# Down projections set between the seven-product pairs, five of eight pairs in seven products, and x kept in DRAM

## The chip, the cores and the metric

The kernel runs on one core of a Trainium2 chip. The core has a matrix engine (TensorE, "PE" in the profile), a vector engine (VectorE, "DVE"), a scalar engine (ScalarE, "ACT"), a general engine (GpSimd, "POOL") and an engine that here only issues transfers (SyncE, "SP"). SP, ACT and POOL can each issue transfers between DRAM and the on-chip memory (SBUF). Matrix products land in eight accumulator banks (PSUM), each of 128 partitions by 512 f32 numbers. The metric is the device time of one execution in microseconds, as the median of several; lower is better.

## The reference

One encoder layer on 256 tokens of width 2048, all in f32. What matters here are its two feed-forward half-steps, which hold more than half of the time. Between them lies a mixing stage (pooling, dilated attention and cross-attention, gated and merged, then `W_out`).

```
x = x + 0.5 * (silu(h @ w_gate) * (h @ w_up)) @ w_down     # h = rmsnorm(x) * gain, d_ff = 5632
h = rmsnorm(x);  x = x + merged(h) @ w_out                  # three gated branches
x = x + 0.5 * (silu(h @ w_gate) * (h @ w_up)) @ w_down     # second half-step, own weights
out = rmsnorm(x) * final_norm
```

## The kernel before

**Products in three parts.** Every f32 operand is split into a high part (`wh`, rounded by an ACT copy to the matrix engine's f32r type) and a low part (`wl`, source minus high part, one DVE subtraction). A product of two 128-row blocks is three matmuls of 128x128 by 128x512: low by high, high by high, high by low. So one weight element costs one ACT pass, one DVE pass and three matmul passes per use.

**Weights.** A weight tile `wf` of 1 MB (128 x 4 x 512) is loaded by SP (L131, L146) into one of 3 buffers, and split into two halves of `wh` and `wl`, which rotate through 4 buffers each (`operands`, L118). An instruction that fills a buffer waits until the matmuls that read the buffer's previous tile are done.

**Feed-forward.** The 5632 hidden columns go in 11 chunks of 512 (`up`, L514). One chunk computes gate and up together, for 8 pairs of 128-row blocks of the 2048 input rows (`pair_gemm`, L221). A pair is either eight block products (two token halves by gate and up by two row blocks) or seven, by a Strassen-type scheme (`SEVEN_PRODUCTS`): the left side holds eight prepared blocks (`seven`), the right side needs the four weight blocks' sums (`sums`, three DVE additions, L153 to L155), which are split as well (`sumsh` on ACT L158, `sumsl` on DVE L159). Only three quarters of the weight tile itself is then split. The products accumulate over the pairs in eight banks q1 to q8, one bank for each product of the scheme. `finish` (L284) combines the banks into gate and up: q1 is copied by ACT, the rest are DVE additions. `SEVEN` = (0, 2, 4, 6): four of eight pairs take seven products, in chunk 0 one pair and in chunk 1 one pair.

**Down.** After silu and product, the chunk's result `u` is turned by the matrix engine (L379, eight 128x128 transposes into two banks) and split into `hT`. `STEPS` puts down(c) after up(c+1): four groups of 512 output columns, each 24 matmuls (4 row blocks, 2 token halves, 3 parts; `gemm`, L182 with L205 to L207) into two banks out of 0 to 3, and then one DVE instruction per token half that scales by 0.5 and adds to `X` (L550). The last two chunks go together in one down step. `X` (128 x 2 x 2048 f32, 16 KB of each partition) stays in SBUF from the first load to the end.

**Order.** The code is traced in program order, with small work items put in a list (`queue`) and taken from it between products (`pop`), and a scheduler then fixes one order for each engine. Each engine runs its own list strictly in order. Tiles with one tag share its buffers: `slot` has 14 of 8 KB (left sides, sums, `hT`), `tmp` 4 of 4 KB, `half` 2 of 2 KB.

Of the kernel before, what the change touches and what calls it, by code (L numbers as in the profile page):

```python
# [17 lines left out]
P = 128  # L18
S = 256
T = S // P  # L20
# [22 lines left out]
SEVEN = (0, 2, 4, 6)  # L43
QUARTERS = {3: (0,), 4: (1,), 5: (2,), 6: (3,)}

STEPS = (0, 1, *sum((((c, c + 1), c + 2) for c in range(9)), ()), (9, 11))
# [20 lines left out]
def tile_encoder_layer(ctx: ExitStack, tc: tile.TileContext, a: dict, out: bass.AP):  # L67
    nc = tc.nc
    sb = ctx.enter_context(tc.tile_pool(name="sb", bufs=1))
    ps = ctx.enter_context(tc.tile_pool(name="ps", bufs=1, space=bass.MemoryType.PSUM))  # L70
    count = [0]
# [149 lines left out]
    def pair_gemm(lhs, w, cols, order, sevens, out, after_seven=(), before=None, pieces=None):  # L221
# [44 lines left out]
        left = sum(7 if j in sevens else 8 for j in order)  # L266
        for j in order:
# [12 lines left out]
            if j == sevens[-1]:  # L280
                queue(*after_seven, soon=True)

    def finish(q, Q, out):


        (c11, c21), (c12, c22) = [[out[n][:, t] for t in range(T)] for n in range(2)]
        if q == "q1":
            nc.scalar.activation(c11, Q["q1"], AF.Copy)
        elif q == "q6":
            Q["v"] = half_tmp([P, CW], F32, "v")  # L290
            nc.vector.tensor_sub(Q["v"], Q["q6"], c11)
            nc.vector.tensor_sub(c21, Q["q7"], Q["v"])
            nc.vector.tensor_add(c12, Q["q5"], Q["v"])
            nc.vector.tensor_sub(c22, Q["q5"], c21)
        elif q not in ("q7", "q5"):
            c = {"q2": c11, "q4": c21, "q3": c12, "q8": c22}[q]
            nc.vector.tensor_add(c, Q[q], c)
# [21 lines left out]
    X = sb.tile([P, T, D], F32, name="X")  # L319
# [15 lines left out]
    def fill_pair(place, src, gain, early=False):  # L335

        seven, L = place
        if not seven:
            tile, half = L

            def part(k):
                j = 2 * half + k
                split(tile[:, 0, j], tile[:, 1, j], src()[:, k], gain[:, k : k + 1])

            return [lambda k=k: part(k) for k in range(2)]
        F = tmp([P, 8, P], "blocks")
# [15 lines left out]
        if early:  # L362
            def one(k):
                own(k)
                parts(slice(2 * k, 2 * k + 2))

            return [lambda: one(0), lambda: one(1), sums, lambda: parts(slice(4, 8))]
# [109 lines left out]
    xts = []  # L477

    def load_x(j):
# [5 lines left out]
        fill = fill_pair(lhs1[j], lambda: xt, g_ffn1[:, 2 * j : 2 * j + 2], early=j == 0)  # L485

        def part(k):
            nc.sync.dma_start(out=xt[:, k : k + step], in_=a["xT"][:, 2 * j + k : 2 * j + k + step, :])
            for f in fill[:1] if step == 1 else fill:
                f()  # L490
            del fill[:1]
            if step == 1 and k == 1:
                queue(*fill)

        def rows(q):
            t, half = q // 2, slice((q % 2) * D // 2, (q % 2 + 1) * D // 2)
            nc.sync.dma_start(out=X[:, t, half], in_=a["x"][t * P : (t + 1) * P, half])

            def squares():
                for n in (2 * (q % 2), 2 * (q % 2) + 1):  # L500
                    sumsq(ssq1, t, n, X[:, t, n * CW : (n + 1) * CW])

            queue(squares)
# [3 lines left out]


    def ffn(lhs, rstd, w_gate, w_up, w_down, after_chunk, operand=None, first=None, side={}):
# [4 lines left out]
        def up(c, after_down, before_down):  # L514
# [3 lines left out]
            kw = dict(before=first, pieces=lambda j: 1 if j == 0 else 2) if opening else {}  # L518
            g, u = tmp([P, T, CW], "gate"), tmp([P, T, CW], "up")
            sevens = SEVEN[-1:] if c == 0 else SEVEN[2::2] if c == 1 else SEVEN  # L520
            order = (1, 0, 3, 2, 5, 4, 6, 7) if after_down else range(KB // 2)
            pair_gemm(lhs, (w_gate, w_up), (c * CW, c * CW), order, sevens, (g, u), turns, **kw)
# [12 lines left out]
            hT[c], turns = turned_lhs(u, (4, 5) if before_down else (0, 1))  # L535
            if before_down:
                queue(*turns)
                turns = []

        def down(chunks, pieces, final):  # L540

            operands = [hT.pop(c) for c in range(*chunks)]
            for n in range(NCH):
                if pieces:
                    queue(*pieces[n], soon=True)
                acc = gemm(operands, w_down, chunks[0] * CW, n * CW, last=final and n == NCH - 1 and first is None)

                def residual(t, n=n, acc=acc):
                    xs = X[:, t, n * CW : (n + 1) * CW]
                    nc.vector.scalar_tensor_tensor(xs, acc[t], 0.5, xs, op0=ALU.mult, op1=ALU.add)  # L550
                    if final:
                        after_chunk(n, t)

                queue(*(lambda t=t, f=residual: f(t) for t in range(T)), soon=True)
                if final and operand is not None:
                    operand(n)

        for i, step in enumerate(STEPS):
            if isinstance(step, int):
                up(step, i > 0 and not isinstance(STEPS[i - 1], int), not isinstance(STEPS[i + 1], int))  # L560
            else:
                down(step, side.get(i, ()), i == len(STEPS) - 1)
# [101 lines left out]
    def side_work():  # L664
        return {len(STEPS) - 1: mem_pieces()}

# [3 lines left out]
    def after1(n, t):  # L670
        src = X[:, :, n * CW : (n + 1) * CW]
        sumsq(ssq2, t, n, src[:, t])

    def operand1(n):
        src = X[:, :, n * CW : (n + 1) * CW]
# [6 lines left out]
        operand1, first=load_x, side=side_work(),  # L682
# [309 lines left out]
    for n in range(NCH):  # L992
        acc = gemm(merged_lhs, a["w_out"], 0, n * CW)
        xs = X[:, :, n * CW : (n + 1) * CW]

        def residual(t, n=n, acc=acc, xs=xs):
            nc.vector.tensor_add(xs[:, t], acc[t], xs[:, t])
            sumsq(ssq3, t, n, xs[:, t])
# [11 lines left out]
    def after2(n, t):  # L1010
# [6 lines left out]
        sumsq(ssq4, t, n, X[:, t, c])  # L1017
        nc.vector.tensor_mul(XG[t][:, c], X[:, t, c], gf[:, c])
# [104 lines left out]
```

## Time and profile before

| | |
|---|---|
| median of 3 runs | 2362.07 us (2361.9 to 2362.45) |
| profiled execution, its own time | 2362.68 us |
| its span, first to last instruction | 2360.9 us |
| PE busy | 2348.3 us, 99% of the span |
| DVE busy | 1854.4 us, 79% |
| ACT busy | 1208.4 us, 51% |
| POOL busy | 0.7 us, no transfers issued |
| granted TensorE clock | 0.999 |

The profile lists, for each engine, the time in which it was busy, the groups of like instructions with the mean duration of one, and what ended each idle stretch. PE's matmuls overlap each other, so the duration of one (some 0.39 us) is not what one costs; the distance between starts is. An engine that is idle costs nothing as long as PE is not kept waiting by it.

### The profile page before, as it was taken

To read this page: it belongs to the slowest core of one execution; us is meant where nothing else is said; L and a number is where in the kernel's file an instruction comes from. 1 tells how busy PE (TensorE), PEld (TensorE's weight loads), DVE (VectorE), ACT (ScalarE), POOL (GpSimd) and SP (SyncE) were. 2 spreads that over 40 slices of the span, in tenths; PEclk is the share of its full clock that TensorE was granted. 3 is DMA by queue.
4 is the path that set the end of the run, shared out by engine and by line. 5 is a ranking of instruction groups with operands and counts; after the bars stand their busy time and mean duration, and the time that the engine had idled before them with its cause. 6 is when DMAs were issued, how large, how long until landed. Compare 5 with 4: busy or idle time off the path is not lost.

```text
span 2360.9 us, 27305 instructions
## 1 busy us (share of the span) xinstructions
PE 2348.3 (99%) x10325; PEld 1890.7 (80%) x10325; DVE 1854.4 (79%) x2282; ACT 1208.4 (51%) x1421; POOL 0.7 (0%) x6
## 2 busy tenths in 40 slices
PE   9999999999999999999999999999999999999998
PEld 7888888888888888888878888787888888888886
DVE  7788888988877676757777656876788888888886
ACT  7555555555556445543344454455555555555554
POOL 0000000000000000000000000000000000000000
PEclk9999999999999999999999999999999999999999
DMA  7555555555574555555545555555555555555563
GB/s 282 200 196 196 196 196 191 187 193 196 195 261 168 194 181 197 183 201 186 189 177 196 169 178 189 186 184 184 187 192 191 192 191 196 196 196 195 194 196 146
DMA packets 92916, 455.89 MB, mean 193 GB/s; under 512 B 10608, under 2 KB 11888, under 8 KB 61552
## 3 DMA queue, kind: packets, MB, share of 16 engines
q1 hardware_dynamic: 92496, 453.10, 56.7%
q8 instruction: 81, 1.33, 0.2%
q10 hardware_dynamic: 288, 1.05, 0.1%
q14 instruction: 51, 0.42, 0.0%
HBM read 452.01 MB, written 2.10 MB: 192 GB/s over the span
## 4 chain that ended last, share of the span: by engine, by line
PE 99%; DVE 0%; DMA 0%; ACT 0%; issue 0%; SPq 0%
PE acc L206 19%; PE acc L207 19%; PE acc L205 19%; PE q L231 13%; PE q L230 13%; PE q L229 13%; PE bank L379 1%; PE bank L822 0%; PE bank L748 0%; PE bank L713 0%; DMA xt<-in_xT 0%; PE bank L806 0%; PE bank L972 0%; PE bank L929 0%; PE bank L952 0%; PE bank L926 0%
## 5 line engine op out<-in xcount | busy, mean ns | idle before, releaser
L110 ACT ACTIVATE wh<-wf 128x1024 fp32r<-128x1024 f32 (+1 forms) x834 | 846.4, 1018 | 978.0 <-PE acc L206 562.5
L111 DVE TENSOR_TENSOR wl<-wf,wh 128x1024 fp32r<-128x1024 f32 (+1 forms) x834 | 970.1, 1169 | 410.0 <-ACT wh L110 405.0
L205 PE MATMUL acc<-wh,lhs 128*128 128x512 f32 x1920 | 769.8, 401 | 0.0
L206 PE MATMUL acc<-wh,lhs 128*128 128x512 f32 x1920 | 759.8, 396 | 0.0
L207 PE MATMUL acc<-wl,lhs 128*128 128x512 f32 x1920 | 758.7, 395 | 0.8 <-DVE wl L111 0.8
L207 PEld LDWEIGHTS acc<-wl,lhs 128*128 128x128 f32 x1920 | 360.4, 188 | 88.8 <-DVE wl L111 2.2
L205 PEld LDWEIGHTS acc<-wh,lhs 128*128 128x128 f32 x1920 | 360.7, 188 | 88.0 <-DVE lhs L111 0.3
L206 PEld LDWEIGHTS acc<-wh,lhs 128*128 128x128 f32 x1920 | 361.0, 188 | 80.2
L231 PE MATMUL q<-wl,lhs 128*128 128x512 f32 x704 | 280.2, 398 | 0.0
L229 PE MATMUL q<-wh,lhs 128*128 128x512 f32 x704 | 278.1, 395 | 0.0
L230 PE MATMUL q<-wh,lhs 128*128 128x512 f32 x704 | 278.0, 395 | 0.0
L158 ACT ACTIVATE sumsh<-sums 128x1024 fp32r<-128x1024 f32 x152 | 160.2, 1054 | 55.0 <-DVE sums L155 51.1
L159 DVE TENSOR_TENSOR sumsl<-sums,sumsh 128x1024 fp32r<-128x1024 f32 x152 | 185.3, 1219 | 0.0
L229 PEld LDWEIGHTS q<-wh,lhs 128*128 128x128 f32 x704 | 132.4, 188 | 32.8
L230 PEld LDWEIGHTS q<-wh,lhs 128*128 128x128 f32 x704 | 132.2, 188 | 33.0
L231 PEld LDWEIGHTS q<-wl,lhs 128*128 128x128 f32 x704 | 132.2, 188 | 31.4 <-DVE wl L111 0.5
L229 PE MATMUL q<-wh,seven 128*128 128x512 f32 x324 | 129.0, 398 | 2.0 <-ACT wh L110 1.5
L231 PE MATMUL q<-wl,seven 128*128 128x512 f32 x324 | 128.3, 397 | 0.0
L230 PE MATMUL q<-wh,seven 128*128 128x512 f32 x324 | 128.1, 396 | 0.0
L230 PE MATMUL q<-sumsh,seven 128*128 128x512 f32 x304 | 120.2, 395 | 0.0
L229 PE MATMUL q<-sumsh,seven 128*128 128x512 f32 x304 | 119.2, 392 | 0.0
L231 PE MATMUL q<-sumsl,seven 128*128 128x512 f32 x304 | 118.6, 391 | 0.0
(157 smaller groups left out, 1562.8 us busy)
## 6 DMA issues: line engine op xcount, KB each, us to landing
wf<-in_w_in SPq DMA_DIRECT2D x100, 1024.0 KB, 4.9
wf<-in_ffn_w_down SPq DMA_DIRECT2D x88, 1024.0 KB, 4.8
wf<-in_ffn_w_gate SPq DMA_DIRECT2D x175, 512.0 KB, 4.2
wf<-in_ffn_w_up SPq DMA_DIRECT2D x175, 512.0 KB, 5.2
wf<-in_w_mem_kv SPq DMA_DIRECT2D x16, 1024.0 KB, 4.8
wf<-in_w_out SPq DMA_DIRECT2D x16, 1024.0 KB, 4.8
wf<-in_w_up_pool SPq DMA_DIRECT2D x8, 1024.0 KB, 4.8
wf<-in_w_up_mem SPq DMA_DIRECT2D x8, 1024.0 KB, 4.8
```

The costliest lines, as they stand in the source:

```text
L110: nc.scalar.activation(hi, src, AF.Copy)
L111: nc.vector.tensor_sub(lo, src, hi.bitcast(F32))
L158: nc.scalar.activation(th[:, r], sums[:, r], AF.Copy)
L159: nc.vector.tensor_sub(tl[:, r], sums[:, r], th[:, r].bitcast(F32))
L205: nc.tensor.matmul(parts[t], lo, wh[:, k % 2], start=kb == 0, stop=False)
L206: nc.tensor.matmul(parts[t], hi, wh[:, k % 2], start=False, stop=False)
L207: nc.tensor.matmul(parts[t], hi, wl[:, k % 2], start=False, stop=kb == n - 1)
L229: nc.tensor.matmul(Q[q], lhsl, wh, start=first, stop=False)
L230: nc.tensor.matmul(Q[q], lhsh, wh, start=False, stop=False)
L231: nc.tensor.matmul(Q[q], lhsh, wl, start=False, stop=final)
L379: nc.tensor.transpose(state["b"][:, k, t * P : (t + 1) * P], src[:, t, c : c + P], ident)
```

## The change

- Five of eight pairs take seven products (`SEVEN` = 1, 2, 3, 5, 6), and they come first in a chunk, the three pairs of eight products last. Chunk 0 takes eight products in all pairs, chunk 1 seven in two pairs. Pair 1's left-side sums are made in chunk 1 instead of chunk 0.
- The down projection of chunk c is cut into eight pieces (4 column groups by 2 token halves, 12 matmuls each), set between products of the seven-product pairs of up(c+2). Each piece accumulates in bank 7 (q8's bank, which the seven-product pairs do not use), is copied by ACT with the factor 0.5 into a 2 KB `half` tile `y`, and POOL issues a transfer of 256 KB that adds `y` to x in DRAM.
- `X` no longer stays in SBUF. x lives in eight DRAM tiles; the first rows are written there by POOL, and the last down step and the `W_out` step read 512 columns at a time into `tmp` tiles by SP (`x_chunk`), add, and write back by POOL (not after the last step).
- The freed space gives `wh` and `wl` 6 buffers each instead of 4.
- Where a bank's chunk had no seven-product pair, ACT copies the bank out instead of a DVE addition.

```diff
-SEVEN = (0, 2, 4, 6)
+SEVEN = (1, 2, 3, 5, 6)
+SUMS = {5: 1}
+HID = DFF // CW
+BETWEEN = 4
...
-        return [sb.tile([P, 2, CW], F32R, tag=tag, bufs=4, name=nm(tag)) for tag in ("wh", "wl")]
+        return [sb.tile([P, 2, CW], F32R, tag=tag, bufs=6, name=nm(tag)) for tag in ("wh", "wl")]
...
+        places = [BETWEEN + (7 * len(sevens) - 1 - BETWEEN) * i // max(1, len(between) - 1) for i in range(len(between))]
...
+                done += 1
+                while places and done >= places[0]:
+                    places.pop(0)
+                    between.pop(0)()
...
-            nc.vector.tensor_add(c, Q[q], c)
+            if "q1" in Q:
+                nc.vector.tensor_add(c, Q[q], c)
+            else:
+                nc.scalar.activation(c, Q[q], AF.Copy)
...
-    X = sb.tile([P, T, D], F32, name="X")
+    XD = [[dr.tile([P, CW], F32, name=f"x{n}{t}") for t in range(T)] for n in range(NCH)]
...
+    def x_chunk(n):
+        xs = tmp([P, T, CW], "xs")
+        for t in range(T):
+            nc.sync.dma_start(out=xs[:, t], in_=XD[n][t])
+        return xs
...
-            sevens = SEVEN[-1:] if c == 0 else SEVEN[2::2] if c == 1 else SEVEN
-            order = (1, 0, 3, 2, 5, 4, 6, 7) if after_down else range(KB // 2)
+            sevens = () if c == 0 else SEVEN[1::2] if c == 1 else SEVEN
+            order = [j for j in range(KB // 2) if j not in sevens]
+            order = range(KB // 2) if c < 2 else [*sevens, *order]
+            between = down_pieces(c - 2) if c > 1 else ()
...
+        def down_pieces(c):
+            L = hT.pop(c)
+            W = {}
+            def piece(n, t):
+                if t == 0:
+                    W[n] = weights(w_down, c * CW, n * CW)
+                b = psum(7, [P, CW], "down")
+                for k in range(4):
+                    wh, wl = W[n][k // 2]
+                    hi = L[:, 0, k, t * P : (t + 1) * P]
+                    lo = L[:, 1, k, t * P : (t + 1) * P]
+                    nc.tensor.matmul(b, lo, wh[:, k % 2], start=k == 0, stop=False)
+                    nc.tensor.matmul(b, hi, wh[:, k % 2], start=False, stop=False)
+                    nc.tensor.matmul(b, hi, wl[:, k % 2], start=False, stop=k == 3)
+                y = half_tmp([P, CW], F32, "y")
+                nc.scalar.activation(y, b, AF.Copy, scale=0.5)
+                nc.gpsimd.dma_start(out=XD[n][t], in_=y, accum_op=ALU.add)
+            return [lambda n=n, t=t: piece(n, t) for n in range(NCH) for t in range(T)]
...
-                    xs = X[:, t, n * CW : (n + 1) * CW]
-                    nc.vector.scalar_tensor_tensor(xs, acc[t], 0.5, xs, op0=ALU.mult, op1=ALU.add)
+            xs = x_chunk(n)
+                nc.vector.scalar_tensor_tensor(xs[:, t], acc[t], 0.5, xs[:, t], op0=ALU.mult, op1=ALU.add)
...
+        nc.gpsimd.dma_start(out=XD[n][t], in_=xs[:, t])
```

**Where it moves instructions.** PE, in the middle of a chunk of the first half-step. Before, the down step stood between two chunks, two banks in turn (`acc`); its first rows, behind the last rows of the chunk's pair of eight products:

```order
L230 MATMUL q_5026<-wh_5286,lhs_86 128x512
L231 MATMUL q_5026<-wl_5287,lhs_86 128x512
L205 MATMUL acc_5321<-wh_5325,lhs_4821 128x512
L206 MATMUL acc_5321<-wh_5325,lhs_4821 128x512
L207 MATMUL acc_5321<-wl_5326,lhs_4821 128x512
```

Now a piece (`down`, 12 matmuls, its first and last three here) stands between the last product of pair 3 and the first of pair 5:

```order
L233 MATMUL q_1442<-wh_1545,seven_94 128x512
L234 MATMUL q_1442<-wl_1546,seven_94 128x512
L597 MATMUL down_1598<-wh_1590,lhs_844 128x512
L598 MATMUL down_1598<-wh_1590,lhs_844 128x512
L599 MATMUL down_1598<-wl_1591,lhs_844 128x512
...
L597 MATMUL down_1598<-wh_1592,lhs_844 128x512
L598 MATMUL down_1598<-wh_1592,lhs_844 128x512
L599 MATMUL down_1598<-wl_1593,lhs_844 128x512
L232 MATMUL q_1392<-wh_1627,seven_95 128x512
```

The twelve matmuls of a piece moved from a stretch of 96 into eight places among the products, and all of them use one bank.

ACT, the second half of the same seven-product pairs. Before, ACT's list there held only splits of weights and sums and, at the end, q1's copy:

```order
L158 ACTIVATE sumsh_5198<-sums_5194 128x1024
L110 ACTIVATE wh_5204<-wf_5191 128x1024
L110 ACTIVATE wh_5206<-wf_5191 128x512
L158 ACTIVATE sumsh_5240<-sums_5236 128x1024
L110 ACTIVATE wh_5246<-wf_5233 128x1024
```

Now the copies out of bank 7 (`y<-down`) stand between the splits:

```order
L601 ACTIVATE y_1611<-down_1598 128x512
L160 ACTIVATE sumsh_1679<-sums_1675 128x1024
L112 ACTIVATE wh_1701<-wf_1699 128x1024
L112 ACTIVATE wh_1703<-wf_1699 128x1024
L601 ACTIVATE y_1660<-down_1647 128x512
L112 ACTIVATE wh_1767<-wf_1764 128x1024
L112 ACTIVATE wh_1769<-wf_1764 128x1024
L300 ACTIVATE gate_1696<-q_1392 128x512
L601 ACTIVATE y_1722<-down_1709 128x512
```

`wf_1699` is the weight tile of the fourth column group of down, `wf_1764` that of pair 0. Each `y` waits for the end of a piece on PE, and what stands below it waits behind it.

SP, the last down step of the first half-step. Before:

```order
L131 DMA wf_5659<-in_ffn_w_down 128x2048
L635 DMA mem_5492<-in_mem 128x2048
L131 DMA wf_5711<-in_ffn_w_down 128x2048
L131 DMA wf_5775<-in_w_mem_kv 128x2048
L131 DMA wf_5815<-in_w_mem_kv 128x2048
```

Now, with the third and fourth group's x (`xs<-x`) and the last two of four column loads of the memory tokens (`xt<-in_memT`) among the first weights of the mixing stage:

```order
L133 DMA wf_5951<-in_ffn_w_down 128x2048
L694 DMA mem_5722<-in_mem 128x2048
L546 DMA xs_5760<-x_87 128x512
L546 DMA xs_5760<-x_88 128x512
L697 DMA xt_5841<-in_memT 128x1024
L133 DMA wf_6015<-in_w_mem_kv 128x2048
L133 DMA wf_6057<-in_w_mem_kv 128x2048
L697 DMA xt_5843<-in_memT 128x1024
L546 DMA xs_5892<-x_89 128x512
```

`xs` and `xt` share the four `tmp` buffers, so these loads wait for a buffer, and the weight loads below them wait on SP behind them.

More of the change, by code (lines that the diff above doesn't have):

```diff
@@ L219, in tile_encoder_layer, with pair_gemm @@
     BANK = {"q1": 0, "q6": 1, "q7": 2, "q5": 3, "q2": 4, "q4": 5, "q3": 6, "q8": 7}
-    def pair_gemm(lhs, w, cols, order, sevens, out, after_seven=(), before=None, pieces=None):
+    def pair_gemm(lhs, w, cols, order, sevens, out, after_seven=(), before=None, pieces=None, between=()):
         pop(1)
@@ L266, in pair_gemm @@
         left = sum(7 if j in sevens else 8 for j in order)
+        done = 0
+        between = list(between)
+        places = [BETWEEN + (7 * len(sevens) - 1 - BETWEEN) * i // max(1, len(between) - 1) for i in range(len(between))]
         for j in order:
@@ L277, in pair_gemm @@
                     finish(q, Q, out)
+                done += 1
+                while places and done >= places[0]:
+                    places.pop(0)
+                    between.pop(0)()
                 if left:
                     pop(left)
-            if j == sevens[-1]:
+            if sevens and j == sevens[-1]:
                 queue(*after_seven, soon=True)
     def finish(q, Q, out):
+        if not out:
+            out.extend(tmp([P, T, CW], name) for name in ("gate", "up"))
         (c11, c21), (c12, c22) = [[out[n][:, t] for t in range(T)] for n in range(2)]
@@ L333, in pair_tiles, with fill_pair @@
         return tiles
[L335 removed]
+    def fill_pair(place, src, gain, own_only=False, own_there=False):
         seven, L = place
@@ L345, in fill_pair, with straight @@
             return [lambda k=k: part(k) for k in range(2)]
+        if own_only:
+            def straight(k):
+                view = src()[:, k].rearrange("p (t c) -> p t c", t=T)
+                split(L[:, 0, 2 * k : 2 * k + 2], L[:, 1, 2 * k : 2 * k + 2], view, gain[:, k : k + 1])
+            return [lambda k=k: straight(k) for k in range(2)]
         F = tmp([P, 8, P], "blocks")
@@ L360, in parts @@
             split(L[:, 0, r], L[:, 1, r], F[:, r])
[L362 to L367, printed above, removed]
+        if own_there:
+            return [lambda: own(0), lambda: own(1), sums, lambda: parts(slice(4, 8))]
         return [lambda: own(0), lambda: own(1), sums, lambda: parts(slice(0, 8))]
@@ L534, in up @@
             queue(*(lambda t=t, f=f: f(t) for t in range(T) for f in (silu, product)), soon=True)
-            hT[c], turns = turned_lhs(u, (4, 5) if before_down else (0, 1))
-            if before_down:
+            hT[c], turns = turned_lhs(u, (0, 1) if c < HID - 1 else (4, 5))
+            if c == HID - 1:
                 queue(*turns)
[L538 to L548, printed above, removed]
-                    xs = X[:, t, n * CW : (n + 1) * CW]
[L550 to L556, printed above, removed]
@@ new lines, in ffn, with residual @@
+        for c in range(HID):
+            up(c)
+        operands = [hT.pop(c) for c in (HID - 2, HID - 1)]
+        for n in range(NCH):
+            if side:
+                queue(*side[n], soon=True)
+            xs = x_chunk(n)
+            acc = gemm(operands, w_down, (HID - 2) * CW, n * CW, last=n == NCH - 1 and first is None)
+            def residual(t, n=n, acc=acc, xs=xs):
+                nc.vector.scalar_tensor_tensor(xs[:, t], acc[t], 0.5, xs[:, t], op0=ALU.mult, op1=ALU.add)
+                after_chunk(n, t, xs)
+            queue(*(lambda t=t, f=residual: f(t) for t in range(T)), soon=True)
+            if operand is not None:
+                operand(n, xs)
```

63 lines of the change are left out of this document (35 added, 28 removed).

## The prediction

> **What bounds the kernel now.** I read the engines' shares first, then the chain of waits, then who keeps PE waiting.
>
> ```profile
> span 2360.9 us, 27305 instructions
> PE 2348.3 (99%) x10325; PEld 1890.7 (80%) x10325; DVE 1854.4 (79%) x2282; ACT 1208.4 (51%) x1421; POOL 0.7 (0%) x6
> PE 99%; DVE 0%; DMA 0%; ACT 0%; issue 0%; SPq 0%
> PE q L229 <- ACT wh L110: 1.5, 2, 1.2
> PE idle L308 <- DVE idle L305: 1.3, 1, 1.3
> PE acc L207 <- DVE wl L111: 0.8, 1, 0.8
> PE q L229 <- DVE gate L297: 0.5, 1, 0.5
> ```
>
> The page gives PE 99% of the span, and the chain that ends last is PE throughout. The last four rows are all of PE's waits (total, times, longest): 4.1 us in the whole kernel. A change therefore gains only what it takes from PE's list, and loses whatever it makes PE wait. What PE's list costs per matmul shows in the timeline and in the table by stretches (length, then busy time and count of PE, PEld, DVE, ACT, POOL):
>
> ```profile
> 394.73 0.39 PE L229 MATMUL q<-wh,lhs 128*128 128x512 f32 x1
> 423.39 0.39 PE L205 MATMUL acc<-wh,lhs 128*128 128x512 f32 x1
> 394.73:423.39 28.66, 28.66 (x124) 23.10 (x123) 24.78 (x28) 16.37 (x18) 0.00 (x0) 1.00 0.58 189
> 423.39:488.62 65.23, 65.23 (x285) 52.57 (x284) 57.30 (x65) 34.37 (x37) 0.00 (x0) 1.00 0.59 194
> ```
>
> Between the first two rows lie 123 matmul starts: 28.66 / 123 = 0.233 us each, at full granted clock (1.00). One whole round (down of one chunk, up of another) is the last row: 65.23 us, PE never idle, 276 matmuls (60 products x 3, and 96) at 0.233 = 64.3, and 8 transposes for the rest. DVE is busy 57.3 of it: 88%, the next bound.
>
> **The change, part by part.**
>
> *Removed from PE.* Per half-step, before: chunks 0 and 1 with 63 products each, nine with 60: 666. Now 64, 62 and nine with 59: 657. Nine products less, three matmuls each, two half-steps: 54 x 0.233 = **12.6 us**. Down and the transposes keep their counts. The round becomes 65.23 - 0.70 = 64.5 us.
>
> *DVE and ACT in a round.* Durations:
>
> ```profile
> L111 DVE TENSOR_TENSOR wl<-wf,wh 128x512 fp32r<-128x512 f32 x4 | 2.7, 682 | 0.0
> L159 DVE TENSOR_TENSOR sumsl<-sums,sumsh 128x1024 fp32r<-128x1024 f32 x8 | 9.7, 1218 | 0.0
> L550 DVE SCALAR_TENSOR_TENSOR X<-acc,X 128x512 f32<-128x512 f32 x8 | 5.2, 682 | 0.0
> L153 DVE TENSOR_TENSOR sums<-wf 128x1024 f32<-128x1024 f32 x4 | 4.9, 1226 | 0.7 <-DMA wf<-in_ffn_w_up 0.6
> L154 DVE TENSOR_TENSOR sums<-sums,wf 128x512 f32<-128x512 f32 x4 | 2.7, 684 | 0.0
> L110 ACT ACTIVATE wh<-wf 128x1024 fp32r<-128x1024 f32 x20 | 21.2, 1060 | 24.8 <-PE q L230 10.7 <-PE acc L206 8.7 <-issue 5.4
> L110 ACT ACTIVATE wh<-wf 128x512 fp32r<-128x512 f32 x4 | 2.5, 620 | 0.8 <-ACT sumsh L158 0.8
> L288 ACT ACTIVATE gate<-q 128x512 f32<-128x512 f32 x1 | 0.6, 577 | 0.0
> ```
>
> One more pair in seven products costs DVE one L153, two L154-like and two L159, and spares half of a 1024-wide L111: 1.23 + 1.37 + 2.44 - 0.54 = +4.5 us. The eight L550 go: -5.2. DVE stays at 57.3 - 0.7 = 56.6 of 64.5, 88% again. ACT gets eight copies like L288 (4.6) and 2 x 1.06 - 0.44: 34.4 + 6.3 = 40.7 of 64.5. So neither is a bound over a round; both are hidden under PE, and the price is nothing as long as each item is in time. That I check along one round, with t = 0 at the first matmul of pair 1, a product 0.70, a piece 12 x 0.233 = 2.80. The pieces then start at 2.8, 8.4, 14.0, 19.6, 25.9, 31.5, 37.1 and 43.4; the pairs of seven end at 46.9.
>
> *The copies out of bank 7 (ACT).* Each must be over before the next piece starts. The hand-over:
>
> ```profile
> 415.45 0.39 PE L231 MATMUL q<-sumsl,seven 128*128 128x512 f32 x1
> 415.95 0.69 DVE L291 TENSOR_TENSOR v<-q,gate 128x512 f32<-128x512 f32 x1 [0.72 <-PE q L231]
> ```
>
> The reader starts 0.50 after the last matmul's start, 0.27 after PE's next slot. A copy is thus over 0.27 + 0.58 = 0.85 us after its piece, and the next piece is 2.8 or 3.5 us away (four or five products). What can stand before it on ACT is a split that waits for its own buffer: the sixth piece's copy stands behind both splits of the fourth column group, and the second of these takes a buffer that this same piece reads to its end at 34.3. So 34.3 + 0.27 + 1.06 + 0.58 = 36.2, against 37.1: **0.9 us to spare**, the narrowest place. Behind that split comes its DVE part (1.22, so 36.9) for a matmul at 39.0. The copy of the last piece stands behind pair 4's and the first of pair 7's splits: 46.9 + 0.27 + 2 x 1.06 + 0.58 = 49.9, against q8's first product at 51.1. Nothing is late by these rows: cost 0; bounds 0 and, if each of 18 rounds loses the 0.9 it has, 16 us.
>
> *Weights for the pieces.* Six `wh` buffers are three tiles ahead instead of two, but a round still has twelve tiles of 1 MB (8 + 4) in 3 `wf` buffers.
>
> ```profile
> wf<-in_ffn_w_down SPq DMA_DIRECT2D x88, 1024.0 KB, 4.8
> bg<-in_b_gate SPq DMA_DIRECT2D x12, 256.0 KB, 3.2
> X<-in_x SPq DMA_DIRECT2D x4, 512.0 KB, 8.3
> xt<-in_memT SPq DMA_DIRECT2D x4, 512.0 KB, 6.8
> ```
>
> A tile comes 4.8 us after its buffer is free; when I follow DVE's new list with the durations above, buffers are free at t = -1.9 (for pair 3, whose sums should start at 6.9) and 6.9 (for the third column group, wanted by ACT at 14.0) leave over 2 us. Cost 0.
>
> *The adding transfers.* No transfer is issued by POOL before, so their time is bounded: 3.2 (the 256 KB row) from below, 8.3 (512 KB, in the crowded opening) from above; bytes move three times, so I take 5. Two `half` buffers alternate, and the tightest reuse is the last piece's: y of the seventh is read at 40.8, its transfer must land, the copy takes 0.6, q8 wants bank 7 at 51.1. So it holds up to 51.1 - 0.7 - 40.8 = **9.6 us**. DVE's `v` waits for the sixth's transfer (36.2 + 5 = 41.2, against q6's end at 42.0) with pair 4's splits behind it, which are wanted from 53 on. Cost 0 at 5 us. They add 8 x 256 KB to 12 MB per round, on engines that are 59% busy.
>
> The Trainium skill, "SBUF — State Buffer", Who interferes with whom, speaks against POOL as issuer: its descriptors cannot be written while a DVE instruction runs in a mode with both ports. But it says that additions of two tensors have no such mode, and a DVE row of 1024 elements here takes 1.22 us and one of 512 0.68, as without one. By the rule the transfers would start without delay, by its opposite up to one DVE row (1.2 us) late; 5 or 6.2 us, either is under 9.6.
>
> *x in DRAM at the edges.* In the last down step `xs` and the memory's `xt` share four buffers, with weights behind them on SP:
>
> ```profile
> 684.32 0.39 PE L205 MATMUL acc<-wh,lhs 128*128 128x512 f32 x1
> 711.07 21.24 SPq L131 DMA_DIRECT2D wf<-in_w_mem_kv x4
> 707.10 0.48 DVE L114 SCALAR_TENSOR_TENSOR lhs<-bank,gains,lhs 128x256 fp32r<-128x256 f32 x1
> 718.37 0.48 DVE L114 SCALAR_TENSOR_TENSOR lhs<-bank,gains,lhs 128x256 fp32r<-128x256 f32 x1
> 726.42 1.66 DVE L114 SCALAR_TENSOR_TENSOR lhs<-xt,gains,lhs 128x256 fp32r<-128x256 f32 x4
> ```
>
> The step starts at 684.3; the first x columns are done with at about 707 (last split of their transposed blocks), the second at about 718. The third `xs` can be issued at 707, before the mixing stage's first weights are due (711.1). The fourth `xt` waits until 718 and lands at 718 + 6.8 = 725; DVE's last use of such columns began at 726. Cost 0, upper bound one landing, 6.8. In the `W_out` step every load has 96 matmuls (22 us) of cover.
>
> *Opening.* Chunk 0 makes no weight sums and one ACT instruction less per first half tile (0.5 us), but PE then stands before the up weights, which land at 9.6 as before:
>
> ```profile
> 9.61 0.63 ACT L110 ACTIVATE wh<-wf 128x512 fp32r<-128x512 f32 x1 [0.72 <-DMA wf<-in_ffn_w_up]
> 11.09 0.44 PE L231 MATMUL q<-wl,seven 128*128 128x512 f32 x1
> ```
>
> Cost 0, between -0.4 and +1. The end keeps its chain.
>
> *Sum.* Against the profiled execution's own 2362.68: -12.6, all else 0, so 2350.1. It ran 0.6 above the median of 2362.07; so **2349.5** for the median.
>
> **The rivals.** *Copies late.* If ACT's list runs later than I reckon, each round loses at the pieces. For: ACT now waits for PE eight times per round, and had no such place. Against: the spare times above. At 0.7 us per round, 18 x 0.7 = 12.6 eats the gain (2362); at the full 0.9 it is 2349.5 + 16 = 2366, at the same place twice 2382.
>
> *Transfers too slow (other side).* One mechanism: y's buffer is not free, ACT stands at the next copy, bank 7 stays full, PE stands at q8. It decides from 9.6 us per adding transfer; each us above costs one per round: at 12 us 18 x 2.4 = 43, so 2393. For: three moves of the bytes, and the 8.3 us row. Against: the 3.2 row.
>
> *Edges.* If the fourth `xt` is late by its landing, 6.8 once: 2356.
>
> *No gain on PE.* If matmuls into one bank were spaced wider than 0.233, the pieces' 96 x 18 would lose. The rows of `acc` take two banks, but a product of `q` accumulates three in a row in one bank at that spacing; so I give it no chance of its own.
>
> **How the numbers follow.** Forecast (2348.5 to 2353) 0.60; edges and small stalls (2353 to 2357) 0.10; copies late 0.18, of which 0.11 ends within 0.2% and 0.07 slower; transfers too slow 0.12, slower. A measurement here can tell about 0.2%, 4.7 us, from no change. So faster 0.70, same 0.11, slower 0.19. The range reaches from 2348 to the 2366 of the copies and leaves out the transfers' case.
>
> **What would show it.** Right: PE 99%, 9711 matmuls of 128x512, a round of 64.5 us with PE not idle, PE's waits below 6 us in all, `y` copies within 0.9 us of their piece, adding transfers landing in 3 to 8 us. Wrong: PE waiting in `down` rows for `y` (copies), in q8's first product for `y` and ACT for transfers (second rival), SP's weight loads waiting behind `xs` near 710 us (edges). A gain above 14 us would mean that PE's spacing changed.

## The result, and the profile after

The changed kernel takes 2348.8 us (median of 4, 2348.36 to 2349.38) against 2362.0 for the kernel before on the same chip (4 runs, 2361.9 to 2362.45): a ratio of 0.9944, with a 95% interval of 0.9932 to 0.9957. It is faster by 13.2 us (0.6%); the forecast was 2349.5.

The page of the changed kernel (engines, and the shares of the chain that ended last):

```profile
span 2347.0 us, 27962 instructions
PE 2334.9 (99%) x10271; PEld 1877.0 (80%) x10271; DVE 1827.2 (78%) x2218; ACT 1311.8 (56%) x1609; POOL 138.5 (6%) x174
PE 99%; DMA 0%; DVE 0%; SPq 0%; ACT 0%; issue 0%; DVEq 0%; ACTq 0%
```

PE still has 99% of the span and 99% of the chain. It runs 54 matmuls fewer than before (10325 then), and the span is 13.9 us shorter. All that PE waits for in this kernel:

```profile
PE q L232 <- ACT wh L112: 2.1, 2, 1.5
PE idle L323 <- DVE idle L320: 1.3, 1, 1.3
```

3.4 us, where it was 4.1. Neither of the two rows has to do with a piece, a copy or a transfer. One round, from the first transpose of a chunk to that of the next, in the table by stretches (columns as in the prediction):

```profile
337.84:402.41 64.57, 64.57 (x282) 51.80 (x281) 56.25 (x62) 39.92 (x47) 6.92 (x8) 1.00 0.77 228
```

PE fills it without a gap; DVE has 56.25 us of it (it had 57.30 of 65.23), ACT 39.92 (34.37), and POOL, which had nothing, 6.92 for eight transfers. The DMA engines are 77% busy where they were 59%. The sixth piece of a round, its copy, the transfer that adds it, and what follows, in rows chosen from the timeline (start, duration, engine; in brackets the idle time before and what ended it):

```profile
259.76 0.40 PE L599 MATMUL down<-wl,lhs 128*128 128x512 f32 x1
260.93 0.58 ACT L601 ACTIVATE y<-down 128x512 f32<-128x512 f32 x1
261.81 0.86 POOL L602 DMA_DIRECT2D x<-y  x1 [5.44 <-ACT y L601]
262.81 0.39 PE L597 MATMUL down<-wh,lhs 128*128 128x512 f32 x1
...
265.85 0.60 ACT L601 ACTIVATE y<-down 128x512 f32<-128x512 f32 x1 [1.96 <-PE down L599]
266.75 0.86 POOL L602 DMA_DIRECT2D x<-y  x1 [4.08 <-ACT y L601]
267.45 0.39 PE L234 MATMUL q<-sumsl,seven 128*128 128x512 f32 x1
268.28 0.69 DVE L303 TENSOR_TENSOR v<-q,gate 128x512 f32<-128x512 f32 x1 [3.43 <-DMA x<-y]
```

The copy is over at 261.51, and the bank is wanted again at 262.81: 1.30 us to spare. DVE stands 3.43 us before `v`, but most of that is the written order: `v` reads q6, whose last matmul starts at 267.45, so it could not start before 267.95 (0.50 us behind the matmul, as in the prediction's rows). Only the last 0.33 us are the transfer: `v` takes the `half` buffer of this sixth `y`, and the transfer lands at 267.97, 6.2 us after its issue. PE does not notice. Nor does it notice ACT's wait before the last `y` of each round, whose buffer the seventh transfer still reads:

```profile
ACT y L601 <- DMA x<-y: 22.6, 18, 3.2
```

That copy is over 0.5 to 3.3 us before bank 7 is wanted by q8. The transfers of this kernel, with the median time from issue to landing at the end:

```profile
wf<-in_ffn_w_down SPq DMA_DIRECT2D x88, 1024.0 KB, 5.3
x<-y POOLq DMA_DIRECT2D x144, 256.0 KB, 6.4
```

### The profile page after: what moved, and what is told of

It is laid out like the page before. It is cut to its first block, busy times and chain, and to the rows that moved or that the text cites. A ratio compares the mean times of both kernels' runs of the same rounds, so it can differ in the third digit from the quotient of the medians.

```text
span 2347.0 us, 27962 instructions
## 1 busy us (share of the span) xinstructions
PE 2334.9 (99%) x10271; PEld 1877.0 (80%) x10271; DVE 1827.2 (78%) x2218; ACT 1311.8 (56%) x1609; POOL 138.5 (6%) x174
## 4 chain that ended last, share of the span: by engine, by line
PE 99%; DMA 0%; DVE 0%; SPq 0%; ACT 0%; issue 0%; DVEq 0%; ACTq 0%
PE acc L208 13%; PE acc L207 13%; PE acc L209 13%; PE q L232 13%; PE q L233 13%; PE q L234 13%; PE down L598 6%; PE down L599 6%; PE down L597 6%; PE bank L396 1%; PE bank L877 0%; PE bank L803 0%; PE bank L768 0%; DMA wf<-in_ffn_w_gate 0%; PE bank L861 0%; PE bank L1027 0%
## 5 line engine op out<-in xcount | busy, mean ns | idle before, releaser
L113 DVE TENSOR_TENSOR wl<-wf,wh 128x1024 fp32r<-128x1024 f32 (+1 forms) x834 | 951.9, 1159 | 362.8 <-ACT wh L112 358.8
L207 PE MATMUL acc<-wh,lhs 128*128 128x512 f32 x1344 | 537.7, 400 | 0.0
L208 PE MATMUL acc<-wh,lhs 128*128 128x512 f32 x1344 | 534.3, 398 | 0.0
L209 PE MATMUL acc<-wl,lhs 128*128 128x512 f32 x1344 | 528.4, 393 | 0.0
L207 PEld LDWEIGHTS acc<-wh,lhs 128*128 128x128 f32 x1344 | 252.5, 188 | 64.7 <-DVE lhs L113 0.3
L209 PEld LDWEIGHTS acc<-wl,lhs 128*128 128x128 f32 x1344 | 252.3, 188 | 60.6
L208 PEld LDWEIGHTS acc<-wh,lhs 128*128 128x128 f32 x1344 | 252.7, 188 | 54.3
L161 DVE TENSOR_TENSOR sumsl<-sums,sumsh 128x1024 fp32r<-128x1024 f32 x188 | 228.1, 1220 | 11.2 <-ACT sumsh L160 10.3
L598 PE MATMUL down<-wh,lhs 128*128 128x512 f32 x576 | 228.5, 397 | 0.0
L599 PE MATMUL down<-wl,lhs 128*128 128x512 f32 x576 | 228.0, 396 | 0.0
L597 PE MATMUL down<-wh,lhs 128*128 128x512 f32 x576 | 227.5, 395 | 0.0
L232 PE MATMUL q<-wh,lhs 128*128 128x512 f32 x528 | 222.1, 421 | 2.1 <-ACT wh L112 2.1
L233 PE MATMUL q<-wh,lhs 128*128 128x512 f32 x528 | 208.3, 395 | 0.0
L602 POOL DMA_DIRECT2D x<-y x144 | 124.6, 865 | 1156.6 <-ACT y L601 1136.3
L601 ACT ACTIVATE y<-down 128x512 f32<-128x512 f32 x144 | 85.3, 592 | 138.1 <-PE down L599 79.7
L233 PE MATMUL q<-sumsh,seven 128*128 128x512 f32 x376 | 148.7, 395 | 0.0
```

The lines of the kernel that those rows point to most:

```text
L113: nc.vector.tensor_sub(lo, src, hi.bitcast(F32))
L161: nc.vector.tensor_sub(tl[:, r], sums[:, r], th[:, r].bitcast(F32))
L207: nc.tensor.matmul(parts[t], lo, wh[:, k % 2], start=kb == 0, stop=False)
L208: nc.tensor.matmul(parts[t], hi, wh[:, k % 2], start=False, stop=False)
L209: nc.tensor.matmul(parts[t], hi, wl[:, k % 2], start=False, stop=kb == n - 1)
L232: nc.tensor.matmul(Q[q], lhsl, wh, start=first, stop=False)
```

## The experiments

Each time stands beside that of the kernel before in the same session (2361.8 to 2362.1 there). "Theory" and "rival" are those of the expectations.

**The fifth pair undone** (four of eight pairs in seven products; the pieces, the transfers and x in DRAM stay).

```diff
-SEVEN = (1, 2, 3, 5, 6)
+SEVEN = (1, 2, 3, 5)
```

> The pieces and the adding transfers stay; the fifth pair in seven products is undone (four of eight), so the eight pieces stand within 27 products and mostly three products (2.1 us) apart instead of four or five. Theory (the gain is the products taken from PE, and moving down costs nothing): 18 products more, 18 x 0.70 = 12.6 us, so 2348.8 + 12.6 = 2361.4, PE's waits as few as with five pairs. Rival (pieces in bank 7, x in DRAM or the six buffers give a part of the gain themselves, or cost something that the fifth pair hides): clearly under 2359 or over 2364.

Measured: 2445.2 us (2443.4 to 2450.3), 84 us over the 2361.4 of the theory and slower than the kernel before by 3.55% (3.40 to 3.71). Eighteen products cannot cost that. Its longest wait of PE; then rows of its timeline around 202 us (POOL, DVE and q6's last matmul), and PE's in the next round:

```profile
PE down L597 <- DVE up L310: 49.4, 16, 4.0
```

```profile
201.58 0.86 POOL L602 DMA_DIRECT2D x<-y  x1 [4.70 <-ACT y L601]
...
202.26 1.23 DVE L113 TENSOR_TENSOR wl<-wf,wh 128x1024 fp32r<-128x1024 f32 x1 [0.21 <-ACT wh L112]
...
205.83 0.40 PE L234 MATMUL q<-sumsl,seven 128*128 128x512 f32 x1
...
210.08 0.69 DVE L303 TENSOR_TENSOR v<-q,gate 128x512 f32<-128x512 f32 x1 [6.59 <-ACT wh L112]
```

```profile
236.81 0.40 PE L234 MATMUL q<-sumsl,seven 128*128 128x512 f32 x1
240.31 0.77 PE L597 MATMUL down<-wh,lhs 128*128 128x512 f32 x1 [3.10 <-DVE up L310]
240.87 0.63 PE L598 MATMUL down<-wh,lhs 128*128 128x512 f32 x1
241.30 0.63 PE L599 MATMUL down<-wl,lhs 128*128 128x512 f32 x1
```

DVE stands for 6.59 us before `v`. Up to 206.33, 0.50 us behind q6's last matmul, it would stand there in any case; the other 3.75 us `v` lacks its buffer, which the transfer issued at 201.58 still reads: it landed 8.2 us after its issue, at 209.8. (The profile names an ACT split, but ACT's last one before was over at 202.2.) By the same working the transfer holds `v` up for 0.33 us in the changed kernel's round above, for 7.6 us in its 18 rounds together, and for 69 us here. Two things make the difference: q6 ends five products after the sixth piece instead of seven (1.4 us), and in this round the transfer takes 2 us longer. Behind `v` stand five splits, and in the next round PE finds bank 7 (q8) not yet added: 3.1 us, 16 times. That the late splits lead to the late addition is read from DVE's list, not shown by itself. The rows after it show a second loss: the next matmuls start 0.43 us apart instead of 0.233.

**The same, with a buffer of its own for `v`.**

```diff
-SEVEN = (1, 2, 3, 5, 6)
+SEVEN = (1, 2, 3, 5)
...
-            Q["v"] = half_tmp([P, CW], F32, "v")
+            Q["v"] = slot([P, CW], F32, "v")
```

> Four pairs in seven products as in the run with the fifth pair undone (2445.2), with one more edit: v no longer takes one of the two half buffers that the y tiles use, but a buffer of the large pool, where one is free with four such pairs. Theory (the 84 us lost there come from DVE's v, which stood 6.6 us a round behind a transfer that still read its buffer, so that the splits behind it came late): the loss goes, and what stays is the price of 18 products, 2348.8 + 12.6 = 2361.4. Rival (the four weight tiles of the pieces within 28 products instead of 35 come too fast for the wf buffers and the DMA): 2425 to 2445, DVE still waits for wf.

Measured: 2371.0 us (2367.3 to 2371.8). 74 of the 84 us come back with this one edit, so the shared buffers were the cause of most of it. `v` now waits for q6 alone:

```profile
DVE v L303 <- PE q L234: 52.5, 20, 2.9
```

The edit also takes ACT's waits for a transfer before the last `y` away (33.4 us in 18 rounds without it, 1.6 us with it), so it shows the sharing as the cause, not `v` by itself. A calm round of this kernel:

```profile
271.53:336.89 65.36, 65.36 (x285) 52.27 (x284) 52.67 (x57) 37.96 (x46) 6.90 (x8) 1.00 0.78 225
```

65.36 - 64.57 = 0.79 us over the changed kernel's round, PE full: the price of one product (0.70), nearly as forecast. 9.6 us are left over; some rounds take 66.5 us, with PE waiting 3.6 us in nine places for a copy `y` and 2.5 us in three for q8's addition. What makes those rounds late I didn't settle. The sign of the rival is there: DVE still stands 75.8 us, 49 times, for the weights `wf` (104.9 us in the run before, 5.8 in the changed kernel), so a part of the rest may be the rival's.

**The fifth pair alone** (the kernel before with one line changed; chunk 1 gets two such pairs by it).

```diff
-SEVEN = (0, 2, 4, 6)
+SEVEN = (1, 2, 3, 5, 6)
```

> The kernel before with five pairs in seven products and nothing else: down stays one stage, x stays in SBUF, four buffers for wh and wl. PE's list loses ten products per half-step (chunk 1 has 62): 60 x 0.233 = 14.0 us, so 2348.1 if nothing else bounds. Theory (the fifth pair needs the rest of the change, since the up stage alone would ask DVE for 37.3 + 4.5 = 41.8 us in 42.9 - 0.7 = 42.2): PE waits for DVE's sumsl and wl in every round; at one to three us each, 2348 + 18 to 54 = 2366 to 2402. Rival (the buffers smooth it over the stages, DVE has 61.8 of 64.5 us over a round): 2348 to 2352, and the moving of down was not needed for the gain.

Measured: 2349.6 us (2348.8 to 2350.7), a ratio of 0.9947 (0.9932 to 0.9962); no difference from the whole change can be told. The theory fell, the rival holds. The round and the waits of PE:

```profile
297.77:362.29 64.52, 64.52 (x283) 52.00 (x281) 61.14 (x70) 35.88 (x39) 0.00 (x0) 1.00 0.58 196
```

```profile
PE q L229 <- DVE seven L111: 2.1, 1, 2.1
PE idle L308 <- DVE idle L305: 1.3, 1, 1.3
PE q L229 <- DVE X L550: 0.9, 1, 0.9
PE q L229 <- ACT wh L110: 0.4, 1, 0.4
```

DVE is busy 61.14 of 64.52 us, 95%, and PE is still full in nearly every round (the third wait, 0.9 us, is the only one inside a round). A likely reason, read from the rows, is that the buffers carry DVE's surplus of the up stage over into the down stage. So the fifth pair by itself gives the gain. The rest without it is the first run above, and costs 83 us. Added to the fifth pair, it brings little or nothing: this kernel's list is 6 matmuls (1.4 us) shorter than the changed kernel's, and 1.5 us of its forecast of 2348.1 are missing, so the rest could be worth a us or two, which these runs can't tell from nothing. What it does bring is room, 56.25 us on DVE instead of 61.14.

**Four buffers instead of six.**

```diff
-        return [sb.tile([P, 2, CW], F32R, tag=tag, bufs=6, name=nm(tag)) for tag in ("wh", "wl")]
+        return [sb.tile([P, 2, CW], F32R, tag=tag, bufs=4, name=nm(tag)) for tag in ("wh", "wl")]
```

> wh and wl get four buffers each again instead of six. The span gained 13.9 us where the 54 matmuls explain 12.6; PE's three gaps of 0.67, 0.98 and 0.42 us (at 51, 1196 and 13 us of the span before) are gone. Theory A (the 0.98 us at 1196 us, in the mixing stage that the change doesn't touch, went because of the two more buffers): PE waits there again for DVE's wl, the time is 2348.8 + 1.0 = 2349.8. Theory B (the buffers are also what keeps the weights of the pieces in time, as a tile for a piece is split well ahead of it): PE waits in the down rows of each round, 18 times some tenths of a us up to one split of 1.06 + 1.16, so 2352 to 2389. Rival (the gap went by the schedule's other changes): no wait near 1190 us and 2348.8.

Measured: 2371.9 us (2368.2 to 2374.6), 23 us slower than with six. The time is within theory B, but of the waits only half are in `down` rows:

```profile
PE down L597 <- DVE up L310: 3.3, 3, 1.5
PE q L234 <- DVE wl L113: 2.7, 8, 0.3
PE q L234 <- DVE sumsl L161: 2.5, 2, 1.9
PE down L599 <- DVE wl L113: 2.1, 7, 0.5
```

These rows make 10.6 of the 23 us; where the rest is lost they don't show. The kernel with the fifth pair alone lives with four buffers. So it is the pieces between the products that need the six. The likely reason, not shown, is that a weight tile for a piece stays in its buffers over two pieces and the products between them. Theory A falls: no wait comes back near 1190 us, so the 0.98 us there went with the order of the work, not with the buffers.

**The time of the transfers doubled.** Each `y` is halved and added twice, with the same sum.

```diff
-                nc.scalar.activation(y, b, AF.Copy, scale=0.5)
+                nc.scalar.activation(y, b, AF.Copy, scale=0.25)
+                nc.gpsimd.dma_start(out=XD[n][t], in_=y, accum_op=ALU.add)
                 nc.gpsimd.dma_start(out=XD[n][t], in_=y, accum_op=ALU.add)
```

> Each piece's y is half as large and is added to x by two transfers instead of one (the sum is the same), so the time for which its buffer is held goes from 6.4 us (median landing now) to about twice that, 12 to 14, over the 9.6 us that I reckoned the buffers tolerate. Theory (the rival of the prediction: ACT stands at the next copy, bank 7 stays full, PE stands): at 13 us at least 18 x (13 - 9.6) = 61 us for the last piece alone, and more where the other pieces, which follow each other by 5.6 us on two buffers (11.2 us per buffer), also come late by about 2 us each: up to 18 x 6 x 2 = 216 more; so 2410 to 2620. Rival (the two transfers run side by side on the DMA engines, landing in little more than one): 2349 to 2352.

Measured: 2609.3 us (2604.0 to 2620.7), 260 us more, at the upper end of the theory. Waits of PE and of POOL:

```profile
PE down L597 <- ACT y L601: 140.0, 60, 8.8
PE bank L396 <- DVE v L303: 42.1, 16, 4.9
```

```profile
POOL x L603 <- DMA x<-y: 870.4, 142, 9.8
```

POOL issues the second transfer only when the first has landed (870.4 / 142 = 6.1 us each), so a `y` is held twice as long. Then PE stands before the pieces for the copy of the piece before, 60 times, and before the transposes for `v`, 16 times. The mechanism of the prediction's second rival is real, and the changed kernel stays clear of it. Its price was far too low: at 12 us per transfer the prediction has 43 us, for one place in a round, where 260 are lost. These waits stand at several places of a round and make 182 us, and PE is slow after many of them (granted clock 0.97 over the run).

**Copies out of bank 7 made longer**, by doing each four times, and then twice.

```diff
                 nc.scalar.activation(y, b, AF.Copy, scale=0.5)
+                nc.scalar.activation(y, b, AF.Copy, scale=0.5)
+                nc.scalar.activation(y, b, AF.Copy, scale=0.5)
+                nc.scalar.activation(y, b, AF.Copy, scale=0.5)
```

> ACT copies each piece out of bank 7 four times instead of once (the same values), so each copy ends 3 x 0.59 = 1.77 us later. In the changed kernel's trace the time from the copy's end to the next use of the bank is 1.16 to 1.29 us at the sixth piece and 1.7 to 2.6 us (medians) at the others. Theory (this spare time is all the cover there is): the sixth piece's follower comes 0.5 us late in each of 18 rounds, the second's just, 9 to 15 us, so 2358 to 2364; more only where splits behind the copies come late too. Rival (PE's products in between leave much more room than I see): 2349. Other rival (ACT's copies were a bound long before): over 2375.

Measured: 2449.0 us (2437.5 to 2456.1), over all but the last rival. PE's main wait and what is behind it:

```profile
PE bank L396 <- DVE v L303: 63.3, 18, 4.5
```

```profile
DVE v L303 <- DMA x<-y: 100.9, 18, 6.6
```

It is not bank 7 that is late, but `v`, and here all of its wait is the transfer, as q6 is long done. The reason is in the written order: the scheduler, which fixes each engine's list, put the seventh and the eighth piece behind the first transposes. So the sixth `y`, whose buffer `v` takes, is sent off (280.1 us in one round) when the transposes have begun (278.0), and the next of them want the bank that `v` must read first. So this run changes two things at once, and says nothing of the spare time of the changed kernel's own order. With one more copy instead of three the order stays:

```diff
                 nc.scalar.activation(y, b, AF.Copy, scale=0.5)
+                nc.scalar.activation(y, b, AF.Copy, scale=0.5)
```

> ACT copies each piece out of bank 7 twice (the same values), 0.59 us more. With four copies the written order changed as well (some 2400 rows of PE's list of 10000 stand elsewhere, pieces move behind the transposes), so that run could not tell the spare time of the changed kernel; with two, PE's list is nearly the same (some 250 rows). Theory (each copy has at least 1.16 us in its typical place before the bank is wanted): nothing is lost, 2348.8, within 2 us. Rival (the covers add up: the later copy makes later transfers, v and the splits behind it are late as with four pairs): 2352 to 2375, PE waits for bank 0 or 1 behind v, or for wl.

Measured: 2351.4 us (2349.9 to 2352.2), 2.6 us more, between the theory (within 2 us) and the rival (from 2352), and less than a measurement tells apart. PE waits 1.0 us in all for bank 7, at two places, but `v` now stands long:

```profile
DVE v L303 <- DMA x<-y: 79.3, 13, 7.8
```

Beyond q6 the transfer holds `v` up for 2.2 to 4.9 us in each round, nearly as long as with four pairs. So this wait is not dear by itself: here the whole loss is 2.6 us, there it was 84. The 0.59 us per copy are nearly covered, as the 1.30 us of the timeline say, and the rounds show how near the edge DVE comes: most take 64.6 us, three of them 65.3 or 65.4.

**Six pairs in seven products**, all at the head of the round.

```diff
-SEVEN = (1, 2, 3, 5, 6)
+SEVEN = (1, 2, 3, 4, 5, 6)
...
-            sevens = () if c == 0 else SEVEN[1::2] if c == 1 else SEVEN
+            sevens = () if c == 0 else (2, 5) if c == 1 else SEVEN
```

> Six of eight pairs in seven products (pair 4 as well) in chunks 2 to 10; chunk 1 keeps two such pairs. Theory (PE's list alone sets the time as long as every other engine is under it): 18 products fewer, 12.6 us, 2348.8 - 12.6 = 2336.2. DVE then has 56.6 + 4.5 = 61.1 us of a round of 63.9, 96%. Rival (DVE becomes the bound because its work can't be placed that evenly): PE waits for DVE's wl and sumsl in every round; from 2.8 us of spare per round downward, each us lost costs 18, so 2340 to 2375.

Measured: 2350.0 us (2348.0 to 2353.3): the rival, all of the 12.6 us lost again. A round with a loss and one without:

```profile
215.48:280.10 64.62, 64.12 (x279) 51.17 (x278) 59.37 (x67) 41.06 (x49) 6.91 (x8) 1.00 0.81 228
280.10:344.01 63.91, 63.91 (x280) 51.16 (x279) 59.90 (x68) 41.27 (x49) 6.91 (x8) 1.00 0.82 231
```

DVE at 93% is not the bound over a round (the second round takes the 63.9 that PE alone needs), but it comes late at some `sumsl` in most rounds.

**Six pairs, spread**: to the edits of the run before comes a pair of eight products before the sixth; the pieces stay among the first five.

```diff
-        places = [BETWEEN + (7 * len(sevens) - 1 - BETWEEN) * i // max(1, len(between) - 1) for i in range(len(between))]
+        places = [BETWEEN + (7 * 5 - 1 - BETWEEN) * i // max(1, len(between) - 1) for i in range(len(between))]
...
-            order = range(KB // 2) if c < 2 else [*sevens, *order]
+            order = range(KB // 2) if c < 2 else [1, 2, 3, 4, 5, 0, 6, 7]
```

> Six pairs in seven products (2350.0 with all six at the head of the round), in the order 1, 2, 3, 4, 5, 0, 6, 7: a pair in eight products, which asks DVE for less, stands before the sixth; the pieces stay within the first 35 products. Theory (DVE's work per round, 59.5 us of 63.9, fits, and only its crowding at the head made PE wait): most of the 13.7 us lost there come back, 2336 to 2343. Rival (93% of the round is too much for DVE wherever it lies): 2348 to 2356.

Measured: 2347.5 us (2345.6 to 2350.1), between theory and rival: 2.4 of 13.7 us come back, within what the runs scatter. So this way of spreading the work does not bring the time back; PE's longest wait is now ACT's `sumsh` (5.4 us, 12 times). That another order would is not excluded.

**Six pairs by turns**: six in chunks 3, 5, 7 and 9, five in the others (`SEVEN` is 1, 2, 3, 4, 5, 6 here too).

```diff
-            sevens = () if c == 0 else SEVEN[1::2] if c == 1 else SEVEN
+            sevens = () if c == 0 else (2, 5) if c == 1 else SEVEN if c % 2 else (1, 2, 3, 5, 6)
```

> The changed kernel with six pairs in seven products in chunks 3, 5, 7 and 9 only, five in the others. Eight products fewer, 8 x 0.70 = 5.6 us. Theory (where all rounds have six, DVE starts each round already late; a round with five lets it catch up): 2348.8 - 5.6 = 2343.2. Rival (a round with six pairs loses what it gains inside itself, by DVE's crowding at its head): 2347 to 2350, rounds of both kinds near 64.6 us.

Measured: 2344.7 us (2344.0 to 2345.5, 5 runs), a ratio of 0.9926 (0.9912 to 0.9940) to the kernel before, and 4.1 us under the changed kernel. Two rounds together, twice:

```profile
273.16:401.58 128.42, 128.42 (x561) 103.03 (x559) 115.84 (x128) 80.03 (x96) 13.81 (x16) 1.00 0.81 230
401.58:530.38 128.80, 128.66 (x561) 102.97 (x560) 114.20 (x127) 79.75 (x96) 13.80 (x16) 1.00 0.80 229
```

128.42 is 64.57 + 63.85, the second one product (0.72) less than the first: PE is full, and the round with six costs what PE's list says. So DVE catches up in the round with five, as the theory has it. Of the 5.6 us forecast 1.5 are missing; some pairs of rounds lose a little, like the second row's 0.4. This is the fastest kernel of the study. Whether the kernel before, with the fifth pair, could take this step too was not run; by its rows DVE would have 61.14 + 4.5 / 2 = 63.4 us of some 64.2 in a round.

**More such pairs in the first chunks**, on the kernel with the fifth pair alone.

```diff
-            sevens = SEVEN[-1:] if c == 0 else SEVEN[2::2] if c == 1 else SEVEN
+            sevens = (SEVEN[-1:] if first else SEVEN[2:]) if c == 0 else SEVEN[1:] if c == 1 and first else SEVEN
```

> The kernel before with five pairs in seven products (2349.6 by itself), and more such pairs in the first two chunks: first half-step's chunk 1 four instead of two; second half-step's chunk 0 three instead of one, chunk 1 five instead of two. Seven products fewer, 7 x 0.70 = 4.9 us. Theory (PE's list sets the time while DVE fits; chunk 0 asks little of DVE): 2349.6 - 4.9 = 2344.7, under both kernels. Rival (two up stages follow each other there without a down stage, so DVE has 41.8 of 42.2 us in chunk 1 and gets late): PE waits for sumsl or wl there, 2346 to 2352.

Measured: 2348.5 us (2346.3 to 2350.5, 5 runs), 1.1 us less than without, with runs 4 us apart. The profiled one took 2346.6, with nearly the same waits of PE as the kernel without these pairs and one more of 1.0 us for `wl`. Whether the missing 3.8 us are lost in chunk 1, as the rival has it, these runs can't tell: inconclusive.

## Why the prediction was right

*PE bounds, and the gain is what leaves its list* (12.6 us). Right. 54 matmuls fewer in the trace, a round of 64.57 us where 64.5 was forecast, PE full in it. The fifth pair alone, without any other part of the change, gives the same time within what the runs tell: that is the cleanest support of this step. It also shows something that the prediction didn't ask: whether the rest of the change was needed for it. It was not.

*DVE and ACT in a round.* Right: 56.25 us for a forecast of 56.6, 39.92 for 40.7.

*Copies out of bank 7.* Right in the result, and a little cautious in the size: at the sixth piece the timeline leaves 1.30 us where I reckoned 0.9. One more copy of 0.59 us cost 2.6 us in the whole kernel, not one round's loss eighteen times. The sign that I gave, copies over within 0.9 us of their piece, holds in the median for the first, third, fifth and seventh piece only: the second and the fourth take 1.1, the sixth 1.5, and the last 2.0 to 4.9, as it waits for the seventh transfer. In single rounds the spare time was smaller than at the sixth piece, once 0.14 us, at a fourth piece. The larger lengthening could not test it, since the order changed with it.

*Weights for the pieces* (0). Right; no PE wait in a `down` row. A `wf` tile of 1 MB takes 5.3 us instead of 4.8. That the six buffers are needed is shown by the run with four: 23 us.

*The adding transfers.* The mechanism was right, a size was off: taken as 5 us, measured 6.4 (median; 4.0 to 9.3), inside the bounds of 3.2 and 8.3 for the median, outside for the longest. It cost PE nothing. Both places that I priced behaved as reckoned. For the last piece's `y` I gave 9.6 us as the limit: the seventh transfer took 9.3 us in one round, and there the copy was over 0.5 us before q8. So the spare time is real, and in one round nearly used up. For `v` I had 0.8 us to spare at 5 us (41.2 against 42.0); with 6.2 us it came 0.33 us late in the round shown, up to 1.6 in others, and what stands behind it was wanted later, as I said. What I didn't price is `v` in a neighbouring kernel: with four pairs the transfer held it up for 69 of the 120 us that DVE stood there in 18 rounds, and 74 of 84 us came back once the buffers were not shared; with four copies it was 100.9 us.

*POOL as the issuer.* The rows to look at are `wl` and `sumsl` in the groups, of the kernel before and of the changed one:

```profile
L111 DVE TENSOR_TENSOR wl<-wf,wh 128x1024 fp32r<-128x1024 f32 (+1 forms) x834 | 970.1, 1169 | 410.0 <-ACT wh L110 405.0
L159 DVE TENSOR_TENSOR sumsl<-sums,sumsh 128x1024 fp32r<-128x1024 f32 x152 | 185.3, 1219 | 0.0
```

```profile
L113 DVE TENSOR_TENSOR wl<-wf,wh 128x1024 fp32r<-128x1024 f32 (+1 forms) x834 | 951.9, 1159 | 362.8 <-ACT wh L112 358.8
L161 DVE TENSOR_TENSOR sumsl<-sums,sumsh 128x1024 fp32r<-128x1024 f32 x188 | 228.1, 1220 | 11.2 <-ACT sumsh L160 10.3
L602 POOL DMA_DIRECT2D x<-y x144 | 124.6, 865 | 1156.6 <-ACT y L601 1136.3 <-issue 12.0 <-ACT wh L112 8.3
```

DVE's rows keep their length (1169 and 1159, 1219 and 1220 ns), and every issue of an adding transfer on POOL takes nearly the same, 856 to 893 ns. By the Trainium skill ("SBUF — State Buffer", Who interferes with whom) a DVE instruction in a mode with both ports and POOL shut each other out, and the sum of two tensors has no such mode; these rows agree with it.

*Edges and opening* (0). Right; no wait of PE behind `xs` or `xt`. In the opening PE's second start comes at 8.68 us instead of 8.45, inside the -0.4 to +1 given.

*What the sum missed.* The span lost 13.9 us, 1.3 more than 54 matmuls. Three short gaps of PE are gone (0.67 us at 51 us, 0.98 at 1196, 0.42 at 13 in the trace before), and the rows of PE's waits fell from 4.1 to 3.4 us. They went with the new order; the run with four buffers shows that the buffers didn't do it at 1196. More can't be said of so small a rest.

*The rivals.* Late copies, slow transfers, late edges and wider spacing of PE each did not come. The first two are real limits: the two copies are at the edge of the one, the doubled transfers beyond the other, at six times the price that I gave.

## What to carry to other kernels

Where one engine is full, count what leaves its list, and then look at the other engines' loads over whole rounds and from round to round: DVE at 95% of a round cost next to nothing in one layout, at 93% of every round it ate the gain in another, and by turns it cost little. When transfers read from a pool of few buffers, look for the other users of that pool on a busy engine, and ask of each wait how much of it the transfer makes and how soon the work behind it is wanted: the same 3 to 4 us before `v` stood in a kernel that lost 84 us and in one that lost 2.6. And try the smallest part of a change by itself; here one line gave the gain as far as the runs can tell, and the rest may be what made room for a next step of 4 us.

## What the runs showed of the hardware

**After a gap, PE is slow for a while.** In the run with four pairs, PE's matmuls start 0.43 us apart instead of 0.233 after gaps between starts of 2.4 to 4.4 us: 13 of 16 such gaps are followed by 5 to 12 slow ones, and none of the five gaps of 1.0 to 1.9 us. With four copies 16 of 18 gaps of 2.4 to 4.9 us are followed by such rows. The granted clock of one round with four pairs is below 1:

```profile
211.67:282.85 71.18, 68.08 (x285) 54.22 (x284) 53.44 (x59) 37.78 (x45) 6.91 (x8) 0.95 0.72 207
```

115 slow matmuls at 0.43 - 0.233 make about 22 us of that kernel's 84. So a wait of 3 us costs PE up to 12 x 0.2 = 2.4 us more than itself. The Trainium skill ("TensorE: Matmul & The Clock Gate", HAM oscillation — how this bites in real kernels) gives idle gaps over about 3.4 us as the danger; here gaps between starts from 2.4 us on (2.0 us idle) were enough, and some of 2.7 to 3.6 us were not.

**A transfer that adds costs the DMA engines about twice a plain one.** The queues of the changed kernel (packets, MB, share of 16 engines):

```profile
q1 hardware_dynamic: 95952, 459.39, 56.7%
q0 software_dynamic: 22656, 44.05, 10.7%
```

SP's queue takes 0.123% of the engines per MB, POOL's 0.243%. Some 6 MB of POOL's are plain writes; if these cost what SP's bytes cost, an adding byte costs about 2.1 times a plain one (an estimate from these two rows). The size of the packets is not the reason: in the trace's packet records an adding packet of 2 KB took 202 ns on the average, a plain one of 2 KB on SP's queue 94. That is how 2 MB more per round, on 12, raise the DMA engines from 59% to 77%.
